# Five PSUM banks for the attention scores, three shared by projections and transposes, the square on ScalarE

## The chip, the cores and the metric

The kernel runs on one core of one Trainium2 chip. The metric is the device time in microseconds, the median of the runs. Five engines work side by side: TensorE (PE, with its weight loads as PEld), VectorE (DVE), ScalarE (ACT), GpSimd (POOL) and SyncE (SP), which issues the DMAs. PSUM, where every matmul writes, has eight banks of 512 float32 columns (128 partitions each); only PE, DVE and ACT reach it.

## The reference

A trunk of two layers over 256 context and 1024 latent tokens of width 1024. Layer 0 is a recurrent branch and a gated unit, layer 1 a short convolution and differential attention; each has an input and an output projection and a LayerNorm. The change touches layer 1 alone:

```python
def diff_attention(q, k, v, lam):
    s = jnp.einsum('bqhmd,bkhmd->bhmqk', q, k).astype(jnp.float32) * (DIFF_HEAD_DIM ** -0.5)
    p = jax.nn.softmax(s, axis=-1)
    a = p[:, :, 0] - lam * p[:, :, 1]
    return jnp.einsum('bhqk,bkhe->bqhe', a.astype(v.dtype), v)
...
    oo = rms_norm(oo, subln_g) * (1.0 - lam_init)
    y_d = oo.reshape(oo.shape[0], oo.shape[1], W) * jax.nn.silu(pp[..., 7 * W:8 * W])
```

There are 4 heads, each with two maps m = 0 and 1, and 1280 keys (context and latent). Each block of 128 query rows has a score matrix of 128 x 1280 per map; the two softmaxes are subtracted, with the second weighted by lambda, and the result is multiplied with V. The rms_norm over the 128 columns of a head needs the square of the attention output.

## The kernel before

**Precision.** A product of float32 is made of three matmuls: each operand is split into a high and a low part (`split`: ACT copies the high part, DVE or POOL subtracts for the low one), and high x high, low x high and high x low are added in PSUM.

**Order.** PE's instructions stand in the order in which the program is written (`manual_schedule`, L55). The orders on DVE, ACT, POOL and, mostly, SP are made by a scheduler of the framework, which also sets the semaphores.

**Layer 1, K and V stage.** After the output of layer 0 (`out0_a`, `out0_b`, `out0_t`, L691 to L745) K and V of the four heads are projected (`k_proj` L775, tile `pk`; `vtile` L204, tile `pv`), ACT copies each out of PSUM, and DMAs write them to DRAM.

**Layer 1, attention loop** (L1029 to L1069). Step i stands for head `i // 8` and the i-th block of 128 queries. In a step PE does:
- `scores(i, 0)` (L952): six matmuls (three pieces of keys, high and low part of Q) into tile `psc`, 128 x 1280. DVE takes the negated maximum (L961, `st`), ACT the exponential with the sum (L963, `e`).
- filler work, for u = 1 the product with V of the two blocks before (`av`, L985, tile `pav`), and every fourth step the norm (`finish1` to `finish3`, L999 to L1022, tiles `pms`, `prs`): L1002 is the square `sq` of `of` on DVE.
- `scores(i, 1)`: the same with the second map; DVE then subtracts the maps (L1059).
- `trans(i - 1)` (L971): ten 128 x 128 transposes of the block before, in three groups j = 0, 1 (four each) and 2 (two) into tile `atr`. ACT copies the high part (`ah`, L138), DVE makes the low part (`al`, L141). Between groups 1 and 2 stands filler work.

**Filler** (`fill`, L933). Other projections are cut into pieces of three matmuls: those of Q and the gate (`proj_qg`, L833, tiles `pq`, `pg8`) and those of the convolution branch (`conv_branch`, L853, tiles `p0` to `p3`; the trace prints all of these as `p`, `pq`, `pg`). `FL` (L929) says how many microseconds of such pieces stand at each place. Each projection fills one bank of 512 columns with 24 matmuls; then ACT or DVE empties it.

**PSUM in this stage.** `psc` has three banks in one buffer, `ps3` (L945) deals two shared `psb` banks and one of its own to `atr`, `pav`, `pms` and `prs` in turn, and projections have two `pb` banks of their own: 3 + 3 + 2.

**Loads at a change of head.** `load_k` (L903) brings K of the next head into the one buffer `kd`, ACT and DVE split it (`k`, L908, L909); this is done once for each map, so the second load waits until the first is split. `load_v` (L912) brings V: ACT makes `vh`, POOL makes `vl`. `load_q` makes `qh` on ACT and `ql` on DVE.

Of the kernel before, what the change touches and what calls it, by code (L numbers as in the profile page):

```python
# [10 lines left out]
F32 = mybir.dt.float32  # L11
F32R = mybir.dt.float32r
AF = mybir.ActivationFunctionType
ALU = mybir.AluOpType
AX = mybir.AxisListType
PSUM = bass.MemoryType.PSUM
# [5 lines left out]
NTOK = CTX + LAT  # L22
# [5 lines left out]
CHUNKS = ((0, 256), (256, 512), (768, 512))  # L28
# [14 lines left out]
def tile_hybrid_trunk(es: ExitStack, tc: tile.TileContext, A, out, scr=None):  # L43
    nc = tc.nc
    V, S, G, T, SY = nc.vector, nc.scalar, nc.gpsimd, nc.tensor, nc.sync

    def pool(name, space=None, **kw):
        if space is not None:
            kw["space"] = space
        return tc.tile_pool(name=name, bufs=1, reuse_waits="tile", **kw)  # L50
# [12 lines left out]
    ps1 = es.enter_context(pool("ps1", PSUM))  # L63
# [147 lines left out]
            if between is not None and k % 2 and k < KT - 1:  # L211
                next(between, None)

    def psb(name="psb"):
        t = ps1.tile([128, 512], F32, name=name, tag="psb", bufs=2)
        return t

    def mod_mm(p, wm, ks):
# [6 lines left out]
    def mod_cols(mb, out, bias, one):  # L225
        p = psb("modcp")
        for i in range(4):
            T.transpose(p[:, 128 * i:128 * i + 128], mb[:, 128 * i:128 * i + 128], ident)
        t = const.tile([128, 4, 2], F32, name="mct", tag="mct", bufs=2)
        V.tensor_reduce(t, p.rearrange("p (i g r) -> p i r g", g=4, r=32)[:, :, 0:2, :], axis=AX.X, op=ALU.add)  # L230
        for o, i0, i1, b, add in zip(out, (0, 2), (2, 4), bias, one):
            V.scalar_tensor_tensor(o, t[:, i0:i1, :], add, b[:, :, None].to_broadcast([128, i1 - i0, 2]),
                                   op0=ALU.add, op1=ALU.add)
# [26 lines left out]
    def pj3(name):  # L260
        t = pj.tile([128, 1536], F32, name=name, tag="pj", bufs=2)
        return t
# [24 lines left out]
    def mod0(k):  # L287
        p = psb("modp")
        wm = WM.pop(k)
        mod_mm(p[:, 0:256], [wm[:, i] for i in range(KT)], range(KT))  # L290
        mb = stp.tile([128, 256], F32, name="mb0", tag="mb0", bufs=2)
        S.activation(mb, p[:, 0:256], AF.Copy)
        return mb

    def hmod(k, mb):
        p = psb("modcp")
        for i in range(2):
            T.transpose(p[:, 128 * i:128 * i + 128], mb[:, 128 * i:128 * i + 128], ident)
        t = const.tile([128, 2, 2], F32, name="mct0", tag="mct", bufs=2)
        V.tensor_reduce(t, p[:, 0:256].rearrange("p (i g r) -> p i r g", g=4, r=32)[:, :, 0:2, :], axis=AX.X,  # L300
                        op=ALU.add)
        V.tensor_tensor(modc[:, k], t, bmodc[:, k, :, None].to_broadcast([128, 2, 2]), op=ALU.add)
        xt = XT.pop(k)
        parts = []
        for c0, n, cnd in ((0, 256, 1), (256, 512, 0), (768, 512, 0)):
            x = xt[:, c0:c0 + n]
            V.tensor_scalar(x, x, modc[:, k, 1, cnd:cnd + 1], modc[:, k, 0, cnd:cnd + 1], op0=ALU.mult, op1=ALU.add)
            hh, hl_ = hs(c0, n)
            S.activation(hh[:, k], x, AF.Copy)
            parts.append((hl_[:, k], x, f32(hh[:, k])))  # L310
            if len(parts) == 2:
                V.tensor_tensor(*parts.pop(0), op=ALU.subtract)
        V.tensor_tensor(*parts.pop(0), op=ALU.subtract)
# [32 lines left out]
    with pool("lrua") as lp, pool("lruc") as lc:  # L346
# [167 lines left out]
        p = pj3("pu")  # L514
# [16 lines left out]
    p = pj3("pz")  # L531
# [6 lines left out]
    for g in range(4):  # L538
        t = gp.tile([128, NTOK], F32, name=f"ss{g}")
        SS.append(t)  # L540
    with pool("sguw") as vw:
# [7 lines left out]
        p = pj3("pu")  # L549
# [48 lines left out]
        p = pj3("pz")  # L598
# [88 lines left out]
    op, po = op_cm.__enter__(), po_cm.__enter__()  # L687
# [61 lines left out]


    mask = [(i + 16) % 32 for i in range(32)]
    pa_cm, pb_cm = pool("pa", PSUM), pool("pb", PSUM)
    pbp, pa = pb_cm.__enter__(), pa_cm.__enter__()

    def pb(name):
        t = pbp.tile([128, 512], F32, name=name, tag="pb", bufs=2)
        return t

    kv_cm = pool("kv", side="right")
    kv = kv_cm.__enter__()  # L760
# [14 lines left out]
    def k_proj(hd, ci):  # L775
        c0, n = CHUNKS[ci]
        p = pb("pk")
        proj1(p[:, 0:n], KW[hd], c0, n)
        S.activation(KF[hd][:, c0:c0 + n], p[:, 0:n], AF.Copy)
# [42 lines left out]
    for t in range(NT):  # L822
        p = pb("pv")
        vtile(p, wv, t)
        vt = kv2.tile([128, 512], F32, name="vt", tag="vt", bufs=3)
        S.activation(vt, p, AF.Copy)
        SY.dma_start(v_d[:, t], vt)
# [112 lines left out]

    KS, VS, QS, AH, OF, SD = {}, {}, {}, {}, {}, {}

    turn = [0]

    def ps3(name):  # L945
        turn[0] += 1
        if turn[0] % 3:
            return psb(name)
        t = pa.tile([128, 512], F32, name=name, tag="ps3", bufs=1)
        return t  # L950

    def scores(i, m, st):  # L952
        hd, pr, u = i // 8, i % 8 // 2, i % 2
        qh, ql = QS[hd, pr]
        cu = slice(128 * u, 128 * u + 128)
        p = pa.tile([128, 1536], F32, name="psc", tag="psc", bufs=1)
        for c, n in CHUNKS:
            o = p[:, 256 + c:256 + c + n]
            T.matmul(o, qh[:, m, cu], KS[m][:, c:c + n], start=True, stop=False)  # L959
            T.matmul(o, ql[:, m, cu], KS[m][:, c:c + n], start=False, stop=True)  # L960
        V.tensor_reduce(st[:, m:m + 1], p[:, 256:1536], axis=AX.X, op=ALU.max, negate=True)  # L961
        e_ = ap.tile([128, NTOK], F32, name="e", tag="e", bufs=3)
        S.activation(e_, p[:, 256:1536], AF.Exp, bias=st[:, m:m + 1], scale=1.0, accum_out=st[:, 2 + m:3 + m])  # L963
        if m == 1:
            V.reciprocal(st[:, 5:6], st[:, 3:4])
            V.scalar_tensor_tensor(st[:, 6:7], st[:, 5:6], st[:, 2:3], nlam, op0=ALU.mult, op1=ALU.mult)
            V.scalar_tensor_tensor(SD[i // 4][:, i % 4:i % 4 + 1], st[:, 2:3], EPS, st[:, 2:3], op0=ALU.mult,
                                   op1=ALU.mult)
        return e_
# [29 lines left out]
    def finish1(hd, half):  # L999
        of = OF.pop((hd, half))  # L1000
        sq = ap.tile([128, 512], F32, name="sq", tag="sq", bufs=1)
        V.tensor_tensor(sq, of, of, op=ALU.mult)  # L1002
        return of, sq

    def finish2(blk, of, sq):
        pm = ps3("pms")
        for i in range(4):
            T.matmul(pm[:, i:i + 1], sq[:, 128 * i:128 * i + 128], onesm[:, 0:1], start=True, stop=True)
        rr = ap.tile([128, 8], F32, name="rr", tag="rr", bufs=2)
        V.scalar_tensor_tensor(rr[:, 0:4], pm[:, 0:4], 1.0 / 128, SD.pop(blk), op0=ALU.mult, op1=ALU.add)  # L1010
        G.tensor_tensor(rr[:, 4:8], rr[:, 0:4], cm05, op=ALU.pow)
        return of, rr
# [16 lines left out]
    for i in range(34):  # L1029
        hd, pr, u = i // 8, i % 8 // 2, i % 2  # L1030
        if i < 32:
            if u == 0:
                QS[hd, pr] = load_q(hd, pr)
            st = ap.tile([128, 8], F32, name="st", tag="st", bufs=3)
# [53 lines left out]
    prj_cm.__exit__(None, None, None)  # L1088
    hl_cm.__exit__(None, None, None)
    pa_cm.__exit__(None, None, None)  # L1090
    pb_cm.__exit__(None, None, None)


    with pool("out1") as op, pool("po1", PSUM) as po:
# [148 lines left out]
```

## Time and profile before

| what | value |
|---|---|
| median of 3 runs | 1166.49 us (1164.43 to 1168.02) |
| profiled execution, own time | 1171.65 us |
| its span, first to last instruction | 1169.9 us |
| mean granted TensorE clock | 0.990 |
| PE busy | 1131.7 us (97%) |
| DVE busy | 736.3 us (63%) |
| ACT busy | 440.3 us (38%) |
| POOL busy | 316.7 us (27%) |

By stage, in us from the start of the span:

| stretch | PE busy | DVE busy | ACT busy | POOL busy | clock |
|---|---|---|---|---|---|
| 0 to 490: layer 0 | 476.56 | 293.70 | 186.77 | 116.53 | 1.00 |
| 490 to 624: K, V, first Q | 134.00 | 39.66 | 34.36 | 48.89 | 1.00 |
| 624 to 1041: attention loop | 403.71 | 297.06 | 198.37 | 87.64 | 0.98 |
| 1041 to 1169.9: rest, output projection | 117.40 | 105.84 | 20.77 | 63.61 | 0.99 |

The profile is one execution. Its own time is the device time of that execution, and the span leaves out what lies around the instructions. A timeline row has the start, the duration, the engine, the line, the operation, output <- inputs and shapes, and in brackets the idle time of the engine just before it, with what ended that idle time. The clock is the share of full speed that PE was granted, 1.00 or 0.50 at any moment (2.4 or 1.2 GHz).

### The profile page before, as it was taken

The numbers are of one execution on the slowest core, as the hardware profiler recorded it, in microseconds if no ns is written. First come the engines' busy times: TensorE is split into PE (matmuls) and PEld (weight loads), VectorE is DVE, ScalarE is ACT, GpSimd is POOL, SyncE is SP. The second block draws the span as 40 slices with busy tenths as digits, with TensorE's granted clock in tenths as the row PEclk, the third lists the DMA queues.
The fourth block names the chain that finished last, engine by engine and source line by source line (L and its number), as shares of the span: only waits on it lengthen the run. The fifth ranks groups of instructions, "written<-read, shape, count | busy, mean of one in ns | idle before, by whom it ended". The sixth has DMA issues, their size and how long they took to land.

```text
span 1169.9 us, 14909 instructions
## 1 busy us (share of the span) xinstructions
PE 1131.7 (97%) x5842; PEld 925.4 (79%) x5842; DVE 736.3 (63%) x1007; ACT 440.3 (38%) x685; POOL 316.7 (27%) x200
## 2 busy tenths in 40 slices
PE   6999999999999999999998999999999899999997
PEld 3767777878888888888887888788788788888776
DVE  5677976943512665644015678786867777738897
ACT  3453654610221333341123555455534454413110
POOL 1111111630240222375014112222212121221971
PEclk9999999999999999999998999999989999999999
DMA  9654552230331534333126213222311410127622
GB/s 371 236 190 141 180 182 70 92 95 1 111 143 45 188 124 139 135 113 131 45 64 194 72 36 94 79 77 64 102 39 45 146 53 20 49 76 249 212 99 82
DMA packets 71095, 133.92 MB, mean 114 GB/s; under 512 B 5857, under 2 KB 34401, under 8 KB 70129
## 3 DMA queue, kind: packets, MB, share of 16 engines
q1 hardware_dynamic: 71024, 132.97, 33.9%
q8 instruction: 46, 0.75, 0.3%
q14 instruction: 25, 0.20, 0.0%
HBM read 105.67 MB, written 27.28 MB: 114 GB/s over the span
## 4 chain that ended last, share of the span: by engine, by line
PE 62%; DVE 7%; DMA 4%; POOL 3%; ACT 2%; issue 2%; SPq 0%; POOLq 0%; DVEq 0%; ACTq 0%
PE p L184 4%; PE p L185 4%; PE p L186 4%; PE pout L666 4%; PE pout L664 4%; PE pout L665 4%; PE pv L208 3%; PE pv L210 3%; PE pv L209 3%; PE psc L959 3%; PE psc L960 3%; PE atr L982 2%; POOL xres L1111 2%; PE pav L994 2%; PE pav L995 2%
## 5 line engine op out<-in xcount | busy, mean ns | idle before, releaser
L141 POOL TENSOR_TENSOR wlo<-wraw,whi 128x512 fp32r<-128x512 f32 x92 | 137.9, 1504 | 478.7 <-ACT whi L138 462.0
L666 PE MATMUL pout<-woh,ylo 128*128 128x512 f32 (+1 forms) x296 | 114.5, 387 | 3.8 <-DVE ylo L141 3.8
L961 DVE TENSOR_REDUCE st<-psc 128x1 f32<-128x1280 f32 x64 | 95.1, 1486 | 32.2 <-PE psc L960 32.1
L664 PE MATMUL pout<-woh,yhi 128*128 128x512 f32 (+1 forms) x296 | 114.8, 388 | 0.2
L665 PE MATMUL pout<-wol,yhi 128*128 128x512 f32 (+1 forms) x296 | 114.1, 385 | 0.0
L963 ACT ACTIVATE e<-psc,st 128x1280 f32<-128x1280 f32 x64 | 85.1, 1330 | 71.9 <-DVE st L961 71.2
L138 ACT ACTIVATE whi<-wraw 128x512 fp32r<-128x512 f32 x92 | 57.2, 627 | 135.9 <-PE p L185 31.6
L184 PE MATMUL p<-hhl,whi 128*128 128x512 f32 x256 | 105.7, 413 | 0.0
L186 PE MATMUL p<-hhl,wlo 128*128 128x512 f32 x256 | 101.5, 396 | 0.0
L185 PE MATMUL p<-hll,whi 128*128 128x512 f32 x256 | 101.2, 395 | 0.0
L959 PE MATMUL psc<-k,qh 128*128 128x512 f32 (+1 forms) x192 | 68.6, 372 | 12.7 <-ACT e L963 12.6
L960 PE MATMUL psc<-k,ql 128*128 128x512 f32 (+1 forms) x192 | 70.0, 365 | 0.0
L666 PEld LDWEIGHTS pout<-woh,ylo 128*128 128x128 f32 x296 | 55.6, 188 | 16.0 <-DVE ylo L141 4.6
L138 ACT ACTIVATE ah<-atr 128x512 fp32r<-128x512 f32 (+1 forms) x96 | 47.0, 525 | 52.2 <-PE atr L982 51.2
L664 PEld LDWEIGHTS pout<-woh,yhi 128*128 128x128 f32 x296 | 55.6, 188 | 12.3 <-issue 0.5
L665 PEld LDWEIGHTS pout<-wol,yhi 128*128 128x128 f32 x296 | 55.7, 188 | 11.4
L138 ACT ACTIVATE yhi<-yraw 128x512 fp32r<-128x512 f32 x36 | 22.5, 630 | 111.4 <-PE pout L665 62.2
L141 DVE TENSOR_TENSOR al<-atr,ah 128x512 fp32r<-128x512 f32 (+1 forms) x96 | 54.6, 593 | 6.1 <-ACT ah L138 5.9
L186 PEld LDWEIGHTS p<-hhl,wlo 128*128 128x128 f32 x256 | 48.7, 190 | 10.8
L185 PEld LDWEIGHTS p<-hll,whi 128*128 128x128 f32 x256 | 49.0, 191 | 8.6
L184 PEld LDWEIGHTS p<-hhl,whi 128*128 128x128 f32 x256 | 48.9, 191 | 8.4
L959 PEld LDWEIGHTS psc<-k,qh 128*128 128x128 f32 x192 | 36.6, 191 | 22.5 <-ACT e L963 17.9
(319 smaller groups left out, 2890.4 us busy)
## 6 DMA issues: line engine op xcount, KB each, us to landing
wraw<-in_w_in_dram SPq DMA_DIRECT2D x44, 512.0 KB, 4.5
wm<-in_w_mod_dram SPq DMA_DIRECT2D x64, 256.0 KB, 2.9
wraw<-in_w_out_dram SPq DMA_DIRECT2D x16, 512.0 KB, 3.6
wm<-in_w_mod_dram SPq DMA_DIRECT2D x7, 1024.0 KB
xt<-in_xcT_dram SPq DMA_DIRECT2D x8, 640.0 KB, 10.1
xres<-in_xc_dram SPq DMA_DIRECT2D x10, 512.0 KB, 3.7
kd<-k_d SPq DMA_DIRECT2D x16, 320.0 KB, 4.7
wvr<-in_w_v_dram SPq DMA_DIRECT2D x8, 512.0 KB, 3.6
```

The costliest lines, as they stand in the source:

```text
L138: S.activation(hi, src, AF.Copy)
L141: le.tensor_tensor(lo, src, f32(hi), op=ALU.subtract)
L184: T.matmul(o, hi[:, k % 4], hh[:, k], start=k == 0, stop=False)
L185: T.matmul(o, hi[:, k % 4], hl_[:, k], start=False, stop=False)
L186: T.matmul(o, lo[:, k % 4], hh[:, k], start=False, stop=k == KT - 1)
L664: T.matmul(o, hi[:, i], wh[:, c], start=first and i == 0, stop=False)
L665: T.matmul(o, hi[:, i], wl[:, c], start=False, stop=False)
L666: T.matmul(o, lo[:, i], wh[:, c], start=False, stop=not first and i == 3)
L959: T.matmul(o, qh[:, m, cu], KS[m][:, c:c + n], start=True, stop=False)
L960: T.matmul(o, ql[:, m, cu], KS[m][:, c:c + n], start=False, stop=True)
L961: V.tensor_reduce(st[:, m:m + 1], p[:, 256:1536], axis=AX.X, op=ALU.max, negate=True)
L963: S.activation(e_, p[:, 256:1536], AF.Exp, bias=st[:, m:m + 1], scale=1.0, accum_out=st[:, 2 + m:3 + m])
```

## The change

- `psb` no longer rotates two buffers. It deals single banks 0 and 1 and, while layer 1 runs, bank 2; it takes the one dealt longest ago, but never the bank of the projection that was started last. Projections (`pb`) and transposes, products and norms (`ps3`) all ask it. So 2 + 3 banks become 3 shared ones.
- The scores get one tile `PSC` of 2560 columns, five banks, for the whole stage: map 0 in columns 0 to 1279, map 1 in 1280 to 2559. The third bank holds the last 256 columns of map 0 and the first 256 of map 1. For map 0 the key pieces are now 512, 512, 256 instead of 256, 512, 512.
- The square of `finish1` becomes an ACT instruction.

```diff
--- before.py
+++ after.py
@@ -211,8 +211,17 @@
             if between is not None and k % 2 and k < KT - 1:
                 next(between, None)
 
-    def psb(name="psb"):
-        t = ps1.tile([128, 512], F32, name=name, tag="psb", bufs=2)
+    bank = {"n": 0, "p": None}
+    last = {0: 0, 1: 0}
+
+    def psb(name="psb", proj=False):
+        bank["n"] += 1
+        free = [b for b in last if b != bank["p"]]
+        b = min(free, key=last.get)
+        last[b] = bank["n"]
+        if proj:
+            bank["p"] = b
+        t = (ps1 if b < 2 else bank["pool"]).tile([128, 512], F32, name=name, tag=f"psb{b}", bufs=1)
         return t
 
     def mod_mm(p, wm, ks):
@@ -749,12 +758,14 @@
 
 
     mask = [(i + 16) % 32 for i in range(32)]
-    pa_cm, pb_cm = pool("pa", PSUM), pool("pb", PSUM)
-    pbp, pa = pb_cm.__enter__(), pa_cm.__enter__()
+    pa_cm = pool("pa", PSUM)
+    pa = pa_cm.__enter__()
+    bank["pool"] = pa
+    last[2] = 0
+    PSC = pa.tile([128, 2 * NTOK], F32, name="psc")
 
     def pb(name):
-        t = pbp.tile([128, 512], F32, name=name, tag="pb", bufs=2)
-        return t
+        return psb(name, True)
 
     kv_cm = pool("kv", side="right")
     kv = kv_cm.__enter__()
@@ -940,27 +951,20 @@
 
     KS, VS, QS, AH, OF, SD = {}, {}, {}, {}, {}, {}
 
-    turn = [0]
-
-    def ps3(name):
-        turn[0] += 1
-        if turn[0] % 3:
-            return psb(name)
-        t = pa.tile([128, 512], F32, name=name, tag="ps3", bufs=1)
-        return t
+    ps3 = psb
 
     def scores(i, m, st):
         hd, pr, u = i // 8, i % 8 // 2, i % 2
         qh, ql = QS[hd, pr]
         cu = slice(128 * u, 128 * u + 128)
-        p = pa.tile([128, 1536], F32, name="psc", tag="psc", bufs=1)
-        for c, n in CHUNKS:
-            o = p[:, 256 + c:256 + c + n]
+        p = PSC[:, NTOK * m:NTOK * m + NTOK]
+        for c, n in (CHUNKS if m else ((0, 512), (512, 512), (1024, 256))):
+            o = p[:, c:c + n]
             T.matmul(o, qh[:, m, cu], KS[m][:, c:c + n], start=True, stop=False)
             T.matmul(o, ql[:, m, cu], KS[m][:, c:c + n], start=False, stop=True)
-        V.tensor_reduce(st[:, m:m + 1], p[:, 256:1536], axis=AX.X, op=ALU.max, negate=True)
+        V.tensor_reduce(st[:, m:m + 1], p, axis=AX.X, op=ALU.max, negate=True)
         e_ = ap.tile([128, NTOK], F32, name="e", tag="e", bufs=3)
-        S.activation(e_, p[:, 256:1536], AF.Exp, bias=st[:, m:m + 1], scale=1.0, accum_out=st[:, 2 + m:3 + m])
+        S.activation(e_, p, AF.Exp, bias=st[:, m:m + 1], scale=1.0, accum_out=st[:, 2 + m:3 + m])
         if m == 1:
             V.reciprocal(st[:, 5:6], st[:, 3:4])
             V.scalar_tensor_tensor(st[:, 6:7], st[:, 5:6], st[:, 2:3], nlam, op0=ALU.mult, op1=ALU.mult)
@@ -999,7 +1003,7 @@
     def finish1(hd, half):
         of = OF.pop((hd, half))
         sq = ap.tile([128, 512], F32, name="sq", tag="sq", bufs=1)
-        V.tensor_tensor(sq, of, of, op=ALU.mult)
+        S.activation(sq, of, AF.Square)
         return of, sq
 
     def finish2(blk, of, sq):
@@ -1088,7 +1092,8 @@
     prj_cm.__exit__(None, None, None)
     hl_cm.__exit__(None, None, None)
     pa_cm.__exit__(None, None, None)
-    pb_cm.__exit__(None, None, None)
+    del last[2]
+    bank["p"] = None
 
 
     with pool("out1") as op, pool("po1", PSUM) as po:
```

No matmul is added or removed, and PE's order is the same but for the three key pieces of map 0. What changes are waits, and the orders that the scheduler gives DVE, ACT, POOL and SP. Three places:

**PE, step 13 of the loop, where the filler goes from the gate projection to the first convolution projection** (`p_...` is its bank, `atr` the last group of transposes; waits name the engine whose semaphore is waited for). Before:

```order
L184 MATMUL p_6349<-hhl,whi 128x512
L185 MATMUL p_6349<-hll,whi 128x512
L186 MATMUL p_6349<-hhl,wlo 128x512 [waits Pool_49]
L184 MATMUL p_6349<-hhl,whi 128x512
L185 MATMUL p_6349<-hll,whi 128x512
L186 MATMUL p_6349<-hhl,wlo 128x512
L982 MATMUL atr<-ident,e 128x128 [waits Activation_49]
L982 MATMUL atr<-ident,e 128x128
```

PE, the same place after:

```order
L184 MATMUL p_6319<-hhl,whi 128x512 [waits DVE_49]
L185 MATMUL p_6319<-hll,whi 128x512
L186 MATMUL p_6319<-hhl,wlo 128x512 [waits Pool_49]
L184 MATMUL p_6319<-hhl,whi 128x512
L185 MATMUL p_6319<-hll,whi 128x512
L186 MATMUL p_6319<-hhl,wlo 128x512
L986 MATMUL atr<-ident,e 128x128 [waits DVE_49]
L986 MATMUL atr<-ident,e 128x128
```

The new projection now waits for DVE, which empties the bank of the step's first transposes (`al`), and the last transposes wait for DVE, which empties the bank of the projection just ended (`sg`, the gate).

**PE, the scores of map 0 that stand right behind that place.** Before:

```order
L959 MATMUL psc<-k_5604,qh 128x256 [waits PE_49,Activation_49]
L960 MATMUL psc<-k_5604,ql 128x256
L959 MATMUL psc<-k_5604,qh 128x512
L960 MATMUL psc<-k_5604,ql 128x512
L959 MATMUL psc<-k_5604,qh 128x512
L960 MATMUL psc<-k_5604,ql 128x512
```

PE, the same scores after:

```order
L963 MATMUL psc<-k_5587,qh 128x512 [waits Activation_49]
L964 MATMUL psc<-k_5587,ql 128x512
L963 MATMUL psc<-k_5587,qh 128x512
L964 MATMUL psc<-k_5587,ql 128x512
L963 MATMUL psc<-k_5587,qh 128x256
L964 MATMUL psc<-k_5587,ql 128x256
```

The piece of 256 keys moved to the end. The first matmul still waits for ACT, and by the count of ACT's semaphore in the built program it is the same instruction as before: the exponential of the scores that precede these, here those of map 1 of the step before, which stand in the other columns.

**ACT, the change from the first to the second head** (`k` is the split of the next head's K, `e` an exponential). Before:

```order
L997 ACTIVATE of<-pav 128x256
L138 ACTIVATE qh<-qd 128x512
L138 ACTIVATE ah<-atr 128x4x128 x2
L963 ACTIVATE e,st<-psc,st 128x1280
L908 ACTIVATE k_5665<-kd 128x1280
L138 ACTIVATE whi<-wraw 128x512
```

ACT, the same place after:

```order
L1001 ACTIVATE of<-pav 128x256
L138 ACTIVATE qh<-qd 128x512
L138 ACTIVATE ah<-atr 128x4x128 x2
L919 ACTIVATE k_5647<-kd 128x1280
L967 ACTIVATE e,st<-psc,st 128x1280
L138 ACTIVATE whi<-wraw 128x512
```

The split of K, which waits for its DMA, moved ahead of the exponential.

## Rows read from the trace of the kernel before

**Rows 1.** Page: busy time of each engine (share of the span), instructions.
```profile
PE 1131.7 (97%) x5842; PEld 925.4 (79%) x5842; DVE 736.3 (63%) x1007; ACT 440.3 (38%) x685; POOL 316.7 (27%) x200
```

**Rows 2.** Waits of PE: us in total, times, longest.
```profile
PE psc L959 <- ACT e L963: 12.6, 9, 3.7
```

**Rows 3.** Timeline of PE: start, us, instruction, idle before and its releaser.
```profile
634.58 0.58 PE L959 MATMUL psc<-k,qh 128*128 128x256 f32 x1 [3.71 <-ACT e L963]
...
712.76 0.39 PE L959 MATMUL psc<-k,qh 128*128 128x256 f32 x1 [1.08 <-ACT e L963]
...
749.22 0.38 PE L959 MATMUL psc<-k,qh 128*128 128x256 f32 x1 [1.94 <-ACT e L963]
...
847.94 0.39 PE L959 MATMUL psc<-k,qh 128*128 128x256 f32 x1 [1.97 <-ACT e L963]
...
926.50 0.38 PE L959 MATMUL psc<-k,qh 128*128 128x256 f32 x1 [2.45 <-ACT e L963]
```

**Rows 4.** Windows: us, busy PE, PEld, DVE, ACT, POOL, clock, DMA share, GB/s.
```profile
633.80:640.60 6.80, 6.02 (x15) 4.86 (x16) 4.66 (x12) 2.64 (x5) 3.87 (x3) 0.50 0.61 184
749.80:753.20 3.40, 3.40 (x12) 2.82 (x11) 3.18 (x4) 1.01 (x2) 0.30 (x1) 0.50 0.03 5
848.80:855.60 6.80, 6.80 (x22) 5.64 (x21) 3.86 (x5) 1.42 (x2) 1.01 (x1) 0.50 0.01 2
927.30:930.70 3.40, 3.40 (x10) 2.62 (x8) 3.36 (x3) 0.00 (x0) 1.28 (x1) 0.50 0.69 192
712.00:719.00 7.00, 6.24 (x43) 5.80 (x43) 6.77 (x10) 4.06 (x7) 0.00 (x0) 1.00 0.21 75
```

**Rows 5.** Timeline of DVE and POOL around the second square.
```profile
743.04 3.27 DVE L1002 TENSOR_TENSOR sq<-of 128x512 f32<-128x512 f32 x1 [1.94 <-ACT of L997]
746.24 1.48 DVE L961 TENSOR_REDUCE st<-psc 128x1 f32<-128x1280 f32 x1
747.64 0.67 DVE L141 TENSOR_TENSOR ql<-qd,qh 128x512 fp32r<-128x512 f32 x1
...
742.81 2.96 POOL L141 TENSOR_TENSOR vl<-vf,vh 128x1280 fp32r<-128x1280 f32 x1 [13.32 <-ACT vh L138]
```

**Rows 6.** Page, groups: line, operation, count, busy us, mean ns, idle before.
```profile
L138 ACT ACTIVATE whi<-wraw 128x512 fp32r<-128x512 f32 x92 | 57.2, 627 | 135.9 <-PE p L185 31.6
```

**Rows 7.** Timeline of PE and DVE in step 13.
```profile
796.21 0.40 PE L184 MATMUL p<-hhl,whi 128*128 128x512 f32 x1
...
797.60 0.38 PE L982 MATMUL atr<-ident,e 128*128 128x128 f32 x2
...
796.13 1.28 DVE L141 TENSOR_TENSOR al<-atr,ah 128x512 fp32r<-128x512 f32 x2
...
799.68 0.68 DVE L850 SCALAR_TENSOR_TENSOR sg<-sg,pg 128x512 f32<-128x512 f32 x1
```

**Rows 8.** Timeline of ACT and PE at the first change of head.
```profile
721.88 1.33 ACT L963 ACTIVATE e<-psc,st 128x1280 f32<-128x1280 f32 x1
...
723.87 1.28 ACT L908 ACTIVATE k<-kd 128x1280 fp32r<-128x1280 f32 x1 [0.57 <-DMA kd<-k_d]
...
724.03 0.28 PE L959 MATMUL psc<-k,qh 128*128 128x256 f32 x1
```

**Rows 9.** Timeline of PE, DVE and ACT at the start of the K stage.
```profile
490.33 0.36 PE L184 MATMUL pk<-hhc,whi 128*128 128x256 f32 x1
...
490.94 0.67 DVE L715 SCALAR_TENSOR_TENSOR xres<-xres,pout 128x512 f32<-128x512 f32 x1
...
499.44 2.21 ACT L733 ACTIVATE h<-ntr,b,g 128x128 f32<-128x128 f32 x6
...
499.53 0.37 PE L184 MATMUL pk<-hhc,whi 128*128 128x256 f32 x1
```

**Rows 10.** Timeline of PE and DVE, the last late pair of the list.
```profile
1020.02 0.39 PE L184 MATMUL p<-hhl,whi 128*128 128x512 f32 x1
...
1020.05 1.28 DVE L141 TENSOR_TENSOR al<-atr,ah 128x512 fp32r<-128x512 f32 x2
```

## The prediction

> **What bounds the kernel now.** The page first: PE is busy 97% of the span, DVE 63% and ACT 38% [rows 1], so time can only come from PE's gaps, from its clock, or from new gaps. The waits of PE come next: the largest item is the scores that wait for an exponential, 12.6 us in nine waits [rows 2]. The timeline of PE shows the five of them that are over 1 us [rows 3]: 3.71, 1.08, 1.94, 1.97 and 2.45. Last the windows: right behind four of the five the granted clock is 0.50, the 1.2 GHz level, for 6.8, 3.4, 6.8 and 3.4 us, while behind the gap of 1.08 it stays at 1.00 [rows 4]. A stretch at half clock loses half its length, so these four gaps cost 3.4 + 1.7 + 3.4 + 1.7 = 10.2 us on top. About 22 us of the attention loop are thus at stake on the winning side. On the losing side stands whatever new wait the shared banks put before PE, which today waits for a bank of transposes or projections hardly at all.
>
> **Part 1, the halves for the scores: 0 us.** Removed would be the wait of a score group for the exponential of the group before. But in the built program the first matmul of each group still waits for just that exponential, for map 1 and for map 0 alike, as the two rows of PE's order show; the reading of ACT's semaphore gives the same instruction as before at every one of them. The order of the key pieces costs nothing, the columns are the same. So of the gaps in [rows 3] this part takes none, and I take 0. The ends are 0 and the whole 22 us.
>
> Here a rule of the Trainium skill bears on the change. The rows show only waits for whole exponentials. PSUM — Partial Sum Buffer, section "PSUM bank collisions raise a hardware error", says that two engines must be kept apart per bank, not per address. By it map 1 has to wait in any case, since its first columns share the third bank with map 0, while map 0 would be free of map 1 in its first two banks; what that would give is the fourth rival, and the sum by it is there.
>
> **Part 2, three banks instead of five: A + B.** I laid the waits of the new PE order over the times of the old trace: for each wait the start of the waiting matmul against the end of the DVE or ACT instruction that frees the bank. Where the second is later, PE must stall. At the start of the K stage there are two such pairs: the first K projection starts at 490.33, but its bank was one of the output projection's and is read by DVE until 490.94 + 0.67 = 491.61, so 1.29 us; the third starts at 499.53, but the fourth of the copies that start at 499.44 ends at 500.94, so 1.41 us [rows 9]. **A = +2.7.**
>
> In the attention loop there are 30 late pairs, from 661.8 us on, the last at 1020.02, where the low part of a transpose is done only 0.71 us later [rows 10]. Together they are 27.65 us late. The worst stands in step 13: the new projection starts at 796.21 and would wait 0.61 us for DVE's first `al`; the last transposes start at 797.60 and would wait for the gate's last read, which ends at 799.68 + 0.68 = 800.36, so 2.76 us [rows 7]. The pattern repeats: two groups of transposes fill the two banks that the projection leaves free, and DVE, with a maximum of 1.48 us ahead of them, empties them about 2 us later than PE comes back. Next in size are 2.10 us (819.0), 2.17 (920.8), 1.85 (710.6), 1.68, 1.56, 1.50, 1.31.
>
> Not all of it adds up. Taken off: 4.76 at the two squares of part 3, where DVE's backlog goes; 1.65 where one late pair covers another (0.61 of the 2.76 above); 3.25 where the stall only comes ahead of one that is already there, 1.08 at 712.76 and 2.17 of the 2.45 at 926.50 [rows 3]; 1.29 at 950.7, where a third square is held. Left is **B = +16.7**. Ends: 22.9 with only the 4.76 off, and 8 if DVE, idle for more than a third of the span, catches up at half of the places. I take 16.7, since a stall moves the work that feeds DVE along with PE, and the pairs stay as late as they are.
>
> **Part 3, the square on ACT: C.** Eight DVE instructions go, eight on ACT come. On ACT the nearest row is a copy of the same shape, 627 ns [rows 6], so 8 x 0.63 = 5.0 us, in front of the copies that free the transposes' banks; ACT is busy 38%, and I take 0 (ends: 0 and +5.0; on DVE 8 x 0.67 = 5.4 could come back, which I also take as 0 but for two places). The two places are the point. The second square takes 3.27 us where a DVE instruction of that shape takes 0.67 (`ql`): it starts at 743.04, just behind POOL's `vl` at 742.81, and ends after `vl` does at 745.77 [rows 5]. So the maximum behind it begins 2.6 us late, the exponential too, and that is the gap of 1.94 at 749.22 with its 1.7 of half clock. The fourth square repeats this before the gap at 847.94, 1.97 and 3.4. With the square on ACT the maximum runs beside `vl`. What is late next is `ql`, of the same kind as the square, and so held until 745.77 in its turn; behind it the first `al` ends near 747.1, the transposes go some 0.8 late, and the scores start near 748.2. That gains 1.0 + 1.7 at the first place and, where `vl` ends earlier against PE, 1.85 + 3.4 at the second. **C = -8.0** (ends 0 and -9.0).
>
> What holds the square is in the rows; that `ql` inherits the lock is my reading of them. SBUF — State Buffer, section "Who interferes with whom", says that a DVE instruction with two SBUF inputs contends with a POOL instruction that reads SBUF, and one with a single SBUF input does not: `ql` has two, `al` (PSUM and SBUF) one. Were `ql` free, the first place would give its whole 1.94 + 1.7, and C would be -8.9.
>
> **Part 4, the scheduler's orders: D.** ACT now splits K of the second head's second map before it takes an exponential. The split started at 723.87, on the landing of its DMA, while the exponential ran at 721.88 [rows 8]. Behind the split it would end at about 723.87 + 1.28 + 1.33 = 726.48, less a little overlap, and the scores that started at 724.03 wait for it: +2.45, and a gap of that size brought 1.7 us of half clock at 926.50, which has this very order. **D = +4.15** (ends 0 and 5.9). The swaps on DVE (the subtraction of the maps ahead of the last `al`) meet no wait with less than 1.8 us to spare: 0.
>
> **The clock: E.** New gaps of 1.9 us and more are those of 2.76 and 2.10; those in [rows 3] of this size each brought 1.7 or 3.4. **E = 2 x 2.55 = +5.1** (ends 0 and four gaps x 3.4 = 13.6).
>
> **The sum**: 2.7 + 16.7 + 0 - 8.0 + 4.15 + 5.1 = +20.65. Against the profiled execution that is 1171.65 + 20.65 = 1192.3; the median of the runs lies 5.2 below that execution, so 1187.
>
> **The rivals.**
> 1. *DVE catches up.* B is 8, D and E nothing: 2.7 + 8 - 8.0 = +2.7, 1169. For it: DVE's idle share. Against it: it is the same maximum, 1.48 us long, that stands before the banks in each step.
> 2. *Nothing is covered.* All 30.35 us of late pairs come, the square gives nothing, D is 5.9, two more half-clock stretches 6.8, and only the 7.2 of gaps already standing behind the late pairs are saved: about +36, 1202. For it: each gap over 1.9 us in the old trace had its half clock.
> 3. *Faster: the square pays more than the banks cost.* The lock of `vl` is the only cause of two of the five gaps; its 8.0 decides as soon as B + D + E is below 5.3. With none of the attention pairs late: 1166.5 - 8.0 + 2.7 = 1161. Against it: the worst pair alone is 2.76.
> 4. *The halves do free map 0* (the bank rule above): the gaps at 712.76, 749.22, 847.94 and 926.50 are all of map 0, 7.44 us and 6.8 of clock, 14.2. D falls to 0; B is then 27.65 - 1.65 - 1.29 - 3.9 (what `ql` leaves of 4.76 is 0.9) = 20.8, and 2.7 + 20.8 - 14.2 + 5.1 = +14.4, 1181. Against it: the built program's wait.
> That the change doesn't do what it says is thus my forecast for part 1.
>
> **How the numbers follow.** The sum above 0.55, the second rival 0.20, the first 0.12, the third 0.08, the fourth 0.05. A measurement here tells about 0.3%, 3.5 us, from no change. The first rival is the case within that, the third is faster, the others are slower: 0.08, 0.12, 0.80. The range goes from the first rival, a little under, to the second with the upper clock term: 1168 to 1206.
>
> **What would show it.** Right: PE's waits list `atr`, `p` and `pg` behind DVE's `al` with some 15 us in all, where [rows 2] has only `psc` behind `e`; `psc` still waits for `e`, at the first change of head too; no gap of 1.9 us behind the second and fourth square, and a maximum that starts some 2.6 us earlier there. Wrong: `psc` no longer in that list (rival 4), or `atr` waiting for less than 8 us (rival 1). DVE held by POOL at other instructions than `ql`, or K's split landing earlier, would break C and D.

## The result, and the profile after

The changed kernel takes 1182.98 us (median of 4 runs, 1180.0 to 1183.81) against 1167.26 us for the kernel before (4 runs, 1164.43 to 1169.36): a ratio of 1.0132, 95% interval 1.0103 to 1.0160. The forecast was 1187 with a range of 1168 to 1206. In all that follows, medians are of all runs of a kernel, while ratios and intervals leave out four slow ones, of 1244 to 4784 us. The profiled execution of after has a time of its own of 1182.98 us, a span of 1181.2 us and a mean clock of 0.992.

The page of after answers [rows 1]: PE is busy for the same time, DVE and ACT have exchanged eight instructions, the squares.

```profile
PE 1133.4 (96%) x5842; PEld 921.8 (78%) x5842; DVE 729.3 (62%) x999; ACT 446.1 (38%) x693; POOL 315.1 (27%) x200
```

PE's waits answer [rows 2] (us in total, times, longest). Before, the stage had little but scores behind an exponential, 12.6 us. After, that is 4.3, and a family of waits for banks stands beside it, 14.2 of some 17 us behind DVE's `al` (waits in layer 0 and in the output projection, and those under 1 us, are left out):

```profile
PE p L184 <- DVE al L141: 5.4, 6, 1.9
PE psc L963 <- ACT e L967: 4.3, 2, 2.5
PE atr L986 <- DVE al L141: 3.8, 4, 1.5
PE pg L184 <- DVE al L141: 3.5, 3, 2.0
...
PE atr L986 <- DVE sg L861: 1.8, 1, 1.8
...
PE pq L184 <- DVE al L141: 1.5, 1, 1.5
PE pk L184 <- ACT h L742: 1.2, 1, 1.2
PE pk L184 <- DVE xres L724: 1.1, 1, 1.1
```

The largest gaps of the attention loop, from PE's timeline (start, us, instruction, idle before and its releaser), answer [rows 3]:

```profile
636.10 0.39 PE L963 MATMUL psc<-k,qh 128*128 128x256 f32 x1 [2.51 <-ACT e L967]
...
729.11 0.77 PE L963 MATMUL psc<-k,qh 128*128 128x512 f32 x1 [1.83 <-ACT e L967]
...
805.87 0.33 PE L986 MATMUL atr<-ident,e 128*128 128x128 f32 x1 [1.82 <-DVE sg L861]
...
829.75 0.50 PE L184 MATMUL p<-hhl,whi 128*128 128x512 f32 x1 [1.91 <-DVE al L141]
...
932.88 0.50 PE L184 MATMUL pg<-hhl,whi 128*128 128x512 f32 x1 [1.97 <-DVE al L141]
```

The windows behind these five gaps (us, busy PE, PEld, DVE, ACT, POOL, clock, DMA share, GB/s) answer [rows 4]: the granted clock is at 0.50 behind three of them and at 1.00 behind the other two.

```profile
637.00:640.40 3.40, 3.40 (x10) 2.66 (x9) 2.81 (x4) 0.98 (x1) 2.19 (x2) 0.50 0.69 204
729.20:732.60 3.40, 3.40 (x9) 2.81 (x10) 3.17 (x6) 0.65 (x2) 1.27 (x1) 0.50 0.52 149
805.90:809.30 3.40, 3.40 (x21) 2.97 (x21) 1.52 (x2) 0.39 (x1) 0.45 (x1) 1.00 0.35 94
829.80:833.20 3.40, 3.40 (x16) 2.81 (x17) 2.34 (x4) 1.37 (x4) 0.00 (x0) 1.00 0.56 128
934.00:937.40 3.40, 3.40 (x11) 2.62 (x10) 3.23 (x4) 1.73 (x4) 0.00 (x0) 0.50 0.32 98
```

**Where the 11.3 us between the two profiled spans come from.** Since PE's order is the same, one and the same matmul can be found in both traces, and the difference of its two starts, taken to the nanosecond, is what has been lost up to there:

| matmul | before | after | lost so far | since the row above |
|---|---|---|---|---|
| first K projection | 490.33 | 491.66 | 1.33 | |
| first scores | 623.97 | 626.80 | 2.83 | both K waits: +2.8 |
| scores behind the first gap | 641.37 | 641.72 | 0.35 | the first gap and its clock: -2.5 |
| scores at the first change of head | 712.76 | 715.89 | 3.13 | bank waits: +2.8 |
| scores behind K's split | 730.11 | 736.76 | 6.66 | K's split before the exponential: +3.5 |
| transposes at the second square | 746.20 | 753.62 | 7.43 | a bank wait: +0.8 |
| projection behind it | 753.57 | 757.26 | 3.69 | the second square: -3.7 |
| product before the fourth square | 836.51 | 846.82 | 10.31 | bank waits: +6.6 |
| norm behind it | 858.09 | 863.24 | 5.14 | the fourth square: -5.2 |
| last scores, end | 1018.60 | 1030.04 | 11.44 | bank waits: +6.3 |

### The profile page after: what moved, and what is told of

Read it like the earlier page. It is cut to its first block, busy times and chain, and to the rows that moved or that the text cites. A ratio compares the mean times of both kernels' runs of the same rounds, so it can differ in the third digit from the quotient of the medians.

```text
span 1181.2 us, 14862 instructions
## 1 busy us (share of the span) xinstructions
PE 1133.4 (96%) x5842; PEld 921.8 (78%) x5842; DVE 729.3 (62%) x999; ACT 446.1 (38%) x693; POOL 315.1 (27%) x200
## 5 line engine op out<-in xcount | busy, mean ns | idle before, releaser
L141 POOL TENSOR_TENSOR wlo<-wraw,whi 128x512 fp32r<-128x512 f32 x92 | 135.5, 1478 | 490.7 <-ACT whi L138 473.9
L986 PE MATMUL atr<-ident,e 128*128 128x128 f32 x320 | 46.6, 276 | 6.7 <-DVE al L141 3.8
```

The costliest lines, as they stand in the source:

```text
L141: le.tensor_tensor(lo, src, f32(hi), op=ALU.subtract)
```

## The experiments

Ratios are against the kernel before, from runs on the same chip as each kernel. The kernel before had a median of 1167.35 us beside experiments 1 to 4, 1168.78 beside 5 and 6, and 1168.55 beside 7, 8 and the second run of the changed kernel. Code and rows are cut to what matters.

**1. The square alone.** Kernel before, one line:

```diff
-        V.tensor_tensor(sq, of, of, op=ALU.mult)
+        S.activation(sq, of, AF.Square)
```

> The kernel before with one edit: the square on ScalarE. Theory (the shared banks cost, the square pays): the gaps of 1.94 and 1.97 us at the second and fourth square and the half clock behind them go, 8 us less, 1159 us (1156 to 1162); DVE's ql at that place takes about 1.5 us instead of 0.67 but hides nothing from PE. Rival (the square's gain in the changed kernel is only a shift: the stalls in front of it moved the square away from the POOL instruction): the square gives nothing by itself, 1167 us (1165 to 1169), and a gap of 1 us or more stays at that place.

Measured: 1159.63 us, ratio 0.9938 (0.9918 to 0.9958). At the second square, DVE's and POOL's timeline:

```profile
741.90 1.49 DVE L961 TENSOR_REDUCE st<-psc 128x1 f32<-128x1280 f32 x1 [2.34 <-PE psc L960]
743.31 1.46 DVE L141 TENSOR_TENSOR ql<-qd,qh 128x512 fp32r<-128x512 f32 x1
...
741.28 2.95 POOL L141 TENSOR_TENSOR vl<-vf,vh 128x1280 fp32r<-128x1280 f32 x1 [13.32 <-ACT vh L138]
...
745.58 0.31 PE L959 MATMUL psc<-k,qh 128*128 128x256 f32 x1
```

The maximum runs beside `vl` at its usual 1.49 us, `ql` inherits the lock, that is, it doesn't end before `vl` has (1.46 us where [rows 5] has 0.67), and the scores start with no gap in front. The theory holds: C is real, and does not need the change of banks.

**2. The changed kernel with the square back on DVE** (the same line, undone).

> The changed kernel with the square back on VectorE. Theory: the collision of square and vl comes back, and with it gaps of about 2 us at the second and fourth square with their half clock: 1183 + 8 = 1191 us (1188 to 1194). Rival (PE comes later at these places because of the bank waits, so the held maximum is hidden): 1183 us (1181 to 1185), the square takes 3 us but no gap over 1 us follows.

Measured: 1190.22 us, ratio 1.0186 (1.0163 to 1.0209). DVE at that place, then PE at the second and fourth square:

```profile
748.13 3.27 DVE L1006 TENSOR_TENSOR sq<-of 128x512 f32<-128x512 f32 x1 [2.02 <-ACT of L1001]
751.32 1.48 DVE L965 TENSOR_REDUCE st<-psc 128x1 f32<-128x1280 f32 x1
...
754.06 0.44 PE L986 MATMUL atr<-ident,e 128*128 128x128 f32 x2 [2.60 <-DVE al L141]
...
860.13 0.44 PE L986 MATMUL atr<-ident,e 128*128 128x128 f32 x2 [1.93 <-DVE al L141]
```

The square's 3.27 us are back, and with three banks they reach PE through the transposes' bank instead of the scores. So the change without its third part would have cost 6 to 8 us more, by the ratios to the two measurements of the changed kernel. The half clock that the theory expected with these gaps did not come in the profiled execution: behind both of them the granted clock was 1.00. It fell behind another gap of the same trace, the 1.88 us of the last transposes in step 13 (start 806.31), behind which it had stayed at 1.00 in the changed kernel:

```profile
807.20:810.50 3.30, 3.30 (x11) 2.64 (x10) 1.18 (x2) 0.00 (x0) 0.00 (x0) 0.50 0.69 210
```

**3. Three shared banks, one score tile.** The changed kernel without the halves (`PSC` goes, and map 0 has the old key pieces again):

```diff
-        p = PSC[:, NTOK * m:NTOK * m + NTOK]
+        p = pa.tile([128, 1536], F32, name="psc", tag="psc", bufs=1)[:, 256:1536]
```

> The changed kernel with the old single score tile of three banks; three banks shared as in the change, two banks unused. Theory (the halves free nothing, since each score group still waits for the exponential just before it): as the changed kernel, 1183 us within 2, and the same waits of psc for e. Rival (the halves do free map 0, and only the banks' cost hides it): without them the gaps before the scores of map 0 come back, 1190 us or more.

Measured: 1178.04 us, ratio 1.0096 (1.0076 to 1.0116), neither number. The waits of `psc` for `e` are 4.9 us, beside 4.3 with the halves, so the halves gain nothing. Since this was 5 us below the changed kernel and not level with it, the changed kernel was run again beside the last runs:

> The changed kernel once more, unchanged, since the version with one score tile in place of the halves came out at 1178.0 us where the same was expected. Theory A (the halves themselves cost something): 1183 us (1181 to 1185) again. Theory B (the two differ only by how often the clock falls to half behind gaps of 1.8 to 2 us, which both have): 1178 to 1181 us.

Measured: 1181.68 us, ratio 1.0116 (1.0098 to 1.0133). The number is that of theory A. But the two intervals overlap, and the gaps of the two traces agree within 0.05 us at every bank wait of the attention loop; the spans are 1.4 us apart, 0.9 of it a norm transpose that waits for POOL's `rr` only with the halves. Whether the halves cost the rest is not settled. That they give nothing is.

**4. Five shared banks, one score tile.** As 3, and the dealing spread over the two unused banks as well:

```diff
-    last[2] = 0
+    last.update({2: 0, 3: 0, 4: 0})
```

> The single score tile of three banks and the change's rule for dealing banks, but over all five others instead of three; square on ScalarE. Theory (the number of shared banks is the cause): no waits of transposes or projections for a bank left, 1159 us like the square alone (1156 to 1162). Rival (the sharing itself or the rule for dealing is the cause: projections and transposes in one pool): still 1170 us or more, with waits of atr, p, pg and pq for al.

Measured: 1167.86 us, ratio 1.0006 (0.9993 to 1.0018). Neither number: the waits for `al` are gone, but 8 us over the square alone are left. PE and DVE in step 13:

```profile
794.61 0.44 PE L985 MATMUL atr<-ident,e 128*128 128x128 f32 x2 [2.58 <-DVE sg L860]
...
792.40 1.55 DVE L1062 SCALAR_TENSOR_TENSOR e<-e,st 128x1280 f32<-128x1280 f32 x1
793.87 0.68 DVE L860 SCALAR_TENSOR_TENSOR sg<-sg,pg 128x512 f32<-128x512 f32 x1
```

With five banks to choose from, the transposes get the very bank of the gate projection that has just ended, and wait until DVE has read it. The rule counts dealings: a projection holds its bank for 24 matmuls, so when it ends, its bank was dealt longest ago.

**5. The rule mended, with five and with three banks:**

```diff
         if proj:
+            if bank["p"] in last:
+                last[bank["p"]] = bank["n"]
             bank["p"] = b
```

> Five shared banks and one score tile as before in this study, but a projection's bank is counted as used last when the projection ends, not when it began. Theory A (the rule is at fault: it counts the dealing, so the bank of a projection that has just ended looks like the oldest and is dealt while its last readers are still at work): the gap of 2.58 us at the last transposes of step 13 and the smaller ones of its kind (0.41, 0.56) go, 1160 us (1157 to 1163), as with the square alone. Theory B (one pool for projections and transposes costs in itself, whatever the rule): 1167 us, with new waits of about the same sum.

> The changed kernel with the same edit: a projection's bank counts as used last when it ends. Theory A (most of the loss is the rule): the waits of atr for sg and of p for al fall by more than half, 1172 us or less. Theory B (three banks are too few under any rule): the waits of atr for a projection's readers (1.82 and 0.38 us) go, but the transposes now wait for the transposes before them instead, 1180 us (1177 to 1184), and at least 12 us of waits for al stay.

Measured with five banks: 1162.29 us, ratio 0.9938 (0.9917 to 0.9960), the same ratio as the square alone; no wait of `atr`, `p`, `pg` or `pq` for a bank is listed. Measured with three: 1179.62 us, ratio 1.0090 (1.0063 to 1.0117). PE's waits there:

```profile
PE p L184 <- DVE al L141: 5.4, 6, 1.9
PE psc L965 <- ACT e L969: 3.6, 2, 2.0
PE pg L184 <- DVE al L141: 3.5, 3, 2.0
PE atr L988 <- DVE al L141: 3.2, 4, 1.1
...
PE pq L184 <- DVE al L141: 1.5, 1, 1.5
```

The wait for `sg` is gone, 13.6 us behind `al` stay. Theory A holds for five banks. For three, theory B has the number, but not in every part: the transposes' own waits for `al` did not grow in exchange, they fell from 3.8 to 3.2 us. The rule costs 0.0068 of the time, some 8 us, where there is a free bank to deal. Where there is none, it is 0.0026 to 0.0042, 3 to 5 us, with overlapping intervals; the waits that left the list come to some 3 us. One pool for both kinds of user costs nothing by itself that the interval, 2.5 us to either side, would show.

**6. K's split without its DMA in front.** The changed kernel, and the kernel of experiment 1, with two buffers for the loads:

```diff
-        kd = ap.tile([128, NTOK], F32, name="kd", tag="kd", bufs=1)
+        kd = ap.tile([128, NTOK], F32, name="kd", tag="kd", bufs=2)
...
-        vf = ap.tile([128, NT, 128], F32, name="vf", tag="kd", bufs=1)
+        vf = ap.tile([128, NT, 128], F32, name="vf", tag="kd", bufs=2)
```

> The changed kernel with two buffers instead of one for the loads of K and V (kd, vf), so that the next load need not wait for the split before it. Theory (ScalarE stands at a split that waits for its DMA, in front of the exponential): the gap of 1.83 us at the first change of head with its half clock of 3.4 us goes, and the gap of 2.51 at the first scores behind the split of V with its 3.4 as well: 1.83 + 1.7 + 2.51 + 1.7 = 7.7 less, 1175 us (1172 to 1178). Rival (the split only moves in front of the copies out of the transposes' banks, which three banks can't bear): 1183 us (1180 to 1187), with larger waits of p and atr for al at the changes of head.

> The kernel before with the square on ScalarE and two buffers for the loads of K and V. Theory (with five banks the copies out of the transposes' banks have time to spare, so that an earlier split costs nothing): the gaps of 2.57 and 2.50 us that the square alone left go, with the one half clock of 3.4 us: 2.57 + 1.7 + 2.50 = 6.8 less, 1153 us (1150 to 1157), faster than both kernels. Rival (the gaps come from ScalarE being busy, not from the DMA): 1159 us, the gaps stay above 1.5.

Measured: the changed kernel 1186.83 us, ratio 1.0163 (1.0139 to 1.0186), the rival's number; the other one 1157.85 us, ratio 0.9905 (0.9885 to 0.9926). In the changed kernel the gap of 1.83 us at 729.11 goes, but the split now stands in front of the copies out of the transposes' banks at the other two changes of head:

```profile
835.05 0.50 PE L184 MATMUL p<-hhl,whi 128*128 128x512 f32 x1 [3.55 <-DVE al L141]
...
941.49 0.79 PE L184 MATMUL pg<-hhl,whi 128*128 128x512 f32 x1 [3.62 <-DVE al L141]
```

There the changed kernel has 1.91 and 1.97. These are ACT's rows ahead of the first of them; in the changed kernel that split came behind the copies, at 831.98:

```profile
830.97 1.25 ACT L919 ACTIVATE k<-kd 128x1280 fp32r<-128x1280 f32 x1
832.13 1.07 ACT L138 ACTIVATE ah<-atr 128x512 fp32r<-128x512 f32 x2
```

So with three banks even 1.3 us more on ACT reach PE. With five the same edit costs nothing there, and the gap of 2.50 that the square alone had left goes. The edit gives some 4 us by the ratios, less than the 6.8 expected, since the first gap of 2.57 only moves: PE now waits 3.08 us for the first `qh`. The cause seemed to be this pair (DVE, POOL):

```profile
623.06 3.43 DVE L767 TENSOR_TENSOR qf<-qf,sh 128x512 f32<-128x512 f32 x1 [1.18 <-POOL qf L766]
...
622.98 2.95 POOL L141 TENSOR_TENSOR vl<-vf,vh 128x1280 fp32r<-128x1280 f32 x1
```

**7. The same with the first head's `vl` on DVE:**

```diff
-        split(vh, vl, vf, le=G)
+        split(vh, vl, vf, le=G if hd else V)
```

> Square on ScalarE, two buffers for the loads of K and V, and for the first head the low part of V on VectorE instead of POOL. Theory (the new gap of 3.08 us at the first scores comes from VectorE's last rotation of Q, held for 3.43 us beside POOL's vl): that instruction takes 1 us or less, the gap shrinks below 1 us, 1155 us (1153 to 1157). Rival (VectorE is then busy with V instead): 1158 us, the gap stays above 2 us.

Measured: 1156.95 us, ratio 0.9899 (0.9883 to 0.9915). DVE, then ACT:

```profile
621.47 1.85 DVE L141 TENSOR_TENSOR vl<-vf,vh 128x1280 fp32r<-128x1280 f32 x1 [0.66 <-ACT vh L138]
623.24 0.68 DVE L767 TENSOR_TENSOR qf<-qf,sh 128x512 f32<-128x512 f32 x1
...
627.45 0.63 ACT L138 ACTIVATE qh<-qd 128x512 fp32r<-128x512 f32 x1 [5.53 <-DMA qd<-q_d]
```

The instruction shrinks to 0.68 as the theory said, but the gap stays (3.59), so the lock was not its cause: `qh` waits for Q's load. SP issues that load here at 621.16, behind K's and a weight's, and in experiment 1 at 619.03, ahead of that weight's. That this order makes the gap is argued; no run changed it alone. The theory was thus half right: the lock was as told, and what PE waited for was not. This is the fastest kernel of the study that has all keys, 11.6 us below before and 25 below the changed kernel; from the one without this edit its interval doesn't separate it.

**8. What freed halves would be worth.** Two kernels that leave out 256 of the 1280 keys, with the mended rule and the square on ACT, so that a score matrix fills two banks and all else has four; they differ in one number:

```diff
-        p = pa.tile([128, 1024], F32, name="psc", tag="psc", bufs=1)
+        p = pa.tile([128, 1024], F32, name="psc", tag="psc", bufs=2)
```

> For the price of the wait that the halves were to remove. Two of the ten key blocks are left out of scores, transposes and product with V, so that a score matrix fills two banks; one score tile, four shared banks, a projection's bank counted as used last when it ends, square on ScalarE. PE has about 17 us less of scores, 15 us of transposes, 12 us of products: 1162 - 44 = 1118 us (1105 to 1130). Each score group waits for the exponential just before it; waits of psc for e of some 7 us are expected by both theories, as with the full keys.

> The same, with two score tiles of two banks each, so that a score group waits for the exponential before the last one, not the last. Theory A (a freed score bank is worth the gaps that it ends): the waits of psc for e go and the time is 7 to 12 us below the version with one tile. Theory B (the maximum and the exponential are then late for the next thing, the transposes that need them): 3 us less or none.

Measured: 1121.12 us with one buffer, ratio 0.9588 (0.9571 to 0.9605), 1113.69 with two, 0.9525 (0.9506 to 0.9543). PE's waits, first with one:

```profile
PE psc L964 <- ACT e L968: 6.6, 5, 3.1
```

and the only ones of the attention loop with two:

```profile
PE atr L987 <- DVE e L1064: 0.4, 1, 0.4
...
PE atr L987 <- DVE sd L972: 0.3, 1, 0.3
```

Theory A holds: 7.4 us, for 6.6 us of gaps and one stretch of 3.4 us at half clock. With two buffers, ten of the score groups start before the exponential of the group in front has ended, by up to 3.7 us. In the traces of before, of after and with one buffer none does. What these two runs don't separate is whether one tile would do if its two ranges shared no bank. In after the first piece of map 0 lies in a bank that map 1 doesn't use, and it waited all the same (729.11 above).

**The four parts**, as differences between ratios to the kernel before, each known to some 0.002 to 0.003: square -0.0062 (experiment 1); one pool with the change's rule, still five banks, +0.0068 (4 less 1); five banks to three +0.0090 (3 less 4); halves +0.0020 (the changed kernel again, less 3), which is not secured. They add up to the 1.0116 of the changed kernel's second measurement because each is taken off the one before.

## Why the prediction was right, and where its terms were off

**The sign and the forecast.** Slower by 1.3%, as forecast, for the reason given: shared banks, with DVE's `al` late. The sum was +20.65 against the profiled execution; its span grew by 11.3. That the time still came within 4 us is in part luck, since two errors cancel. The sum is 9.3 too high, most of it by E (5.1) and by a gain at the first scores that it doesn't have (2.5). And the step from the execution to the median (5.2 down) did not apply: the profiled execution of after is at its median, that of before was 5.2 above its own.

**Part 1, 0 us: right as to gain.** `psc` still waits for `e`, also for map 0 at the first change of head. Experiment 8 shows that this was a matter of how the space is declared: with two buffers, the wait goes and 7.4 us with it. For the fourth rival the Trainium skill was cited (PSUM — Partial Sum Buffer, section "PSUM bank collisions raise a hardware error"): engines must be kept apart per bank. No run here tests that rule. It did not decide: the program made a score group wait for the whole tile, also where it shares no bank with the group in front.

**A, +2.7: right.** Gaps of 1.10 and 1.22 us, 2.8 by the starts.

**B, +16.7: right in sum.** By the table of starts, what is left of the 11.1 us between the third row and the last, once K's split (3.5) and the two squares (-8.9, with 0.8 of bank wait just ahead of the first) are taken out, is some 15.7. The worst pair was put at 2.76 behind one of 0.61; it came as 1.82 behind 0.50. The next in size (2.10, 2.17, 1.85) came as 1.91, 1.97 and, behind one of 0.28, 1.12. What the prediction had wrong in kind is its cause for that pair: it is the rule, not the number of banks, since it stays at 2.58 us with five (experiment 4) and goes with the mended rule.

**C, -8.0: right**, by the starts (-8.1 with that 0.8), by the square alone (-7.7 in the medians) and by its undoing (+6 to +8). That `ql` inherits the lock was a reading then and is a row now, in after too (start, us, instruction):

```profile
750.10 1.49 DVE L965 TENSOR_REDUCE st<-psc 128x1 f32<-128x1280 f32 x1 [2.43 <-PE psc L964]
751.51 1.46 DVE L141 TENSOR_TENSOR ql<-qd,qh 128x512 fp32r<-128x512 f32 x1
...
749.48 2.94 POOL L141 TENSOR_TENSOR vl<-vf,vh 128x1280 fp32r<-128x1280 f32 x1 [13.42 <-ACT vh L138]
```

`ql` ends 0.55 us after `vl`, as the square did in [rows 5], and the maximum in front of it keeps its 1.49. This agrees with the rule cited from the Trainium skill (SBUF — State Buffer, section "Who interferes with whom"): of DVE's instructions those with two SBUF inputs contend with a POOL instruction that reads SBUF. The other half of what the prediction says there, that one with a single SBUF input does not, fits `al`, which took at most 0.69 us in all 96 places of after. It is too wide for other operations, as the last section shows.

**D, +4.15: right in kind, 0.6 too large.** ACT in after, with the split's wait for its DMA in brackets:

```profile
726.48 1.27 ACT L919 ACTIVATE k<-kd 128x1280 fp32r<-128x1280 f32 x1 [1.51 <-DMA kd<-k_d]
727.65 1.31 ACT L967 ACTIVATE e<-psc,st 128x1280 f32<-128x1280 f32 x1
```

The gap is 1.83 instead of 2.45, with the 3.4 us of half clock.

**E, +5.1: wrong, nothing came.** This is the step that failed: "those in [rows 3] of this size each brought 1.7 or 3.4". Behind 1.82 and 1.91 in after the clock stays at 1.00. The second run of the changed kernel has the same gaps (1.74 at 730.56, 1.91 at 829.76, 1.98 at 932.91), and the clock behind them is this:

```profile
730.60:734.00 3.40, 3.40 (x16) 2.83 (x17) 3.17 (x6) 0.77 (x3) 1.29 (x1) 1.00 0.53 153
...
829.80:833.20 3.40, 3.40 (x16) 2.81 (x17) 2.34 (x4) 1.42 (x4) 0.00 (x0) 1.00 0.50 119
932.90:936.30 3.40, 3.39 (x16) 2.79 (x17) 2.73 (x5) 3.05 (x5) 0.00 (x0) 1.00 0.24 77
```

Two of the three that fell to half speed in one execution kept full speed in the other. Behind the gap of step 13 it stayed at 1.00 in both, and fell behind the same gap in experiment 2 (1.88 us) and in the changed kernel of experiment 6 (1.83 us). So in these traces a gap of this size has a chance of half clock, not a price. Over all fourteen traces, the attention loop has 31 gaps of 1.6 to 3.6 us besides the first one, and the clock fell behind 11 of them. Only the first gap, 1.98 to 3.71 us in thirteen traces, brought half clock every time. The old trace had a row that said so and that the prediction passed over, in the output projection:

```profile
1089.08 0.50 PE L666 MATMUL pout<-woh,ylo 128*128 128x512 f32 x1 [2.09 <-DVE ylo L141]
```

Behind these 2.09 us the clock of before stayed at 1.00. Four of four in its attention loop was a high draw. The mean clocks of the other executions of before bear this out: in 37 of them, on three chips, it was 0.988 to 0.997, with a median of 0.994 and only two below the 0.990 of the profiled one, and the executions with a lower clock were the longer ones (a median of 1170.27 us at 0.992 and less, 1166.8 at 0.995 and more). That is also why that execution lay above its median, as far as times and clocks without a trace can show it.

**Not in the sum:** -2.5 at the first scores, where the gap was 2.51 us instead of 3.71 and the half clock 3.4 us instead of 6.8. The gap hangs on V's load, and comes out between 2.0 and 3.7 in the traces of kernels that have this order; the part of it that the change causes can't be told from chance.

**The rivals.** The first (DVE catches up) and second (nothing is covered) are out by B. A sign that was named for the first did appear: `atr` waits for 6.5 us in all, 3.8 of it for `al`, which is less than 8. It was a poor sign, since more of the waits than expected stand at `p`, `pg` and `pq`; behind `al` there are 14.2 us in all, where the prediction had some 15. The third asked which is larger, lock or banks: the lock gave what it said, banks and rule more than twice that. The fourth is out by the waits of `psc`.

## What to carry to other kernels

Lay the waits of a changed program over the times of the old trace: the large pairs that come late that way came late on the chip, at the same matmuls and 0.2 to 0.9 us shorter. The half clock behind a gap in one profile is a chance, so it belongs in the range and not at full price in the sum. Before space is taken from one stage to give another room to run ahead, read in the built program whether the wait is gone; two ranges of one tile didn't free it, and in the kernels with fewer keys two tiles did, for 7.4 us. A rule that deals buffers must count from the release and not from the dealing, as soon as some users hold theirs longer than others.

## What the runs showed that was not expected

**A gap costs PE more than its idle time.** At 698.63 the timeline of after shows 1.21 us idle, and the transposes behind that piece of work start 1.46 us later against the kernel before:

```profile
698.63 0.51 PE L184 MATMUL p<-hhl,whi 128*128 128x512 f32 x1 [1.21 <-DVE al L141]
698.97 0.39 PE L185 MATMUL p<-hll,whi 128*128 128x512 f32 x1
699.20 0.39 PE L186 MATMUL p<-hhl,wlo 128*128 128x512 f32 x1
```

Running matmuls of this shape start 0.23 us apart and are shown as 0.39 long, so an idle time counts only from 0.16 after the start that was missed; and the second one behind the gap starts 0.34 after the first, 0.11 more. That makes 0.25 to 0.27 us per gap of a projection, and the same was seen at 789.06 (1.59 for 1.35), 829.75 (2.15 for 1.91) and 932.88 (2.21 for 1.97). Over fourteen bank waits of 0.38 to 1.97 us it is some 3 us that the list of waits doesn't show.

**The lock of DVE and POOL reaches more than one kind of instruction.** It held the square for 3.27 us, `ql` for 1.46 and the rotation of Q for 3.43. Each ended 0.5 to 0.6 us after `vl`, where the same shapes take 0.67 to 0.69 alone. Two inputs in SBUF are not needed: in the trace of before, the TENSOR_SCALAR `xres<-xres,bso` (L717) on DVE has one input tile of 128x1024 and two values per partition. It takes 0.81 us nine times, and 1.77 at 402.68, beside POOL's `wlo`, which runs from 402.62 to 403.91; here too the end comes 0.54 us after POOL's. TENSOR_REDUCE out of PSUM was not held: 1.49 us beside `vl`, as elsewhere.
